# Weighted values of 64-wide heads with the probabilities stationary, the norm as a diagonal product, and reordered leading groups and gates

## The chip, the cores and the metric

The kernel runs on one core of one Trainium2 chip. The metric is the device time of one execution in microseconds (us), the median of three runs. The engines are TensorE (PE, with its weight loads as PEld), VectorE (DVE), ScalarE (ACT), GpSimd (POOL) and SyncE (SP), which here only issues DMAs.

## The reference

Two transformer blocks on 256 tokens of width 2048, all f32. The first block has two kinds of 64-wide attention heads side by side, sixteen each; each kind's 1024 outputs are normed together, and both go through one output matrix:

```python
h = rmsnorm(x, pre_mix_g[l]); proj = h @ w_in[l]
o_a = swa_sink_attention(q_a, k_a, v_a, sinks[l])         # 16 heads, 2 kv heads, window 128, sink in the sum
o_b = forgetting_attention(q_b, k_b, v_b, log_f)          # 16 heads, logit += c[t]-c[s], c = cumsum(log f)
o_a = rmsnorm(o_a.reshape(B, S, D_SWA), grp_swa_g[l])
o_b = rmsnorm(o_b.reshape(B, S, D_FOX), grp_fox_g[l])
mix = jnp.concatenate([o_a, o_b], axis=-1) @ w_out[l]
x = x + rmsnorm(mix, post_mix_g[l])                       # then a gated feed-forward with a short convolution
```

In both attentions a head's output is `p @ v` with `p = exp(s - m) / sum`. The second block mixes stick-breaking attention, a gated linear attention in chunks and a gated spatial unit, then attends to 256 memory rows, adds the residual and ends with a norm of x.

## The kernel before

**Layout.** Activations lie feature-major, as (128, k-tile, 256 tokens). A big product splits activations and weights into a high and a low f32r half and sums three of the four partial products: for one k-tile and one tile of 128 outputs, a product of 256 columns with the low weights (line 248) and one of 512 columns with the high weights (line 249). A group is two tiles over 16 k-tiles; one k-tile of a group is one step. `as_chunk` (lines 281 to 283) makes outputs by token instead, three products a k-tile and half.

**Weights.** `WeightStream` loads units of up to 128x1024 into four raw buffers, all DMAs on SP. ACT copies the high half (line 110), DVE subtracts for the low half (line 117), and PE uses the unit two units later. A unit is four k-tiles of a group. A raw buffer is loaded again when DVE is done with it.

**Order.** One program order per engine is written out by hand: side work runs as Python generators (`push`, `step`), each advanced once every so many steps; `yield n` means n steps later. `drain` advances them with no step of the stream between. PSUM has two-buffer tags P (groups) and S (scores) and single banks T and O.

**Attention.** `attn64` (line 402) takes heads in pairs. Scores go to S (line 475), DVE adds the bias and takes the maximum (483), ACT exponentiates with the sum accumulated (416), DVE takes the reciprocal and scales the probabilities, 128 and 256 columns per head (424 to 427), PE transposes three 128x128 blocks into T (434), ACT copies them out (437). `values` then makes the head's output feature-major in O, values stationary (64 columns) and transposed probabilities moved:

```python
o = self.p("O")
for h in (h0, h0 + 1):
    r, pt = (h % 2) * 64, weighted.pop(h)
    nc.tensor.matmul(o[r:r + 64, 0:S], vf(h, 0), pt[:, 0:S], start=True, stop=False)
    nc.tensor.matmul(o[r:r + 64, P:S], vf(h, 1), pt[:, S:S + P], start=False, stop=True)
```

ACT copies O out (455) and squares it (463); POOL sums the squares (465). For the forgetting heads ("fox") the pairs run while their keys arrive, but the values of the second values chunk (`v_chunk(2)`, flag `foxv`) come last, so their eight pairs are released together, one step apart, in `mix_tail`.

**Norm.** `group_norm_split` (line 499) sums over partitions with products by ones (`rms`, 328), takes the inverse root on ACT and DVE, multiplies the eight tiles on DVE and POOL in turn (508), and splits each into halves (217, 225) for the output matrix. `mix_tail` runs three output groups over the first eight k-tiles, drains the side work, and goes on with the other eight.

**Gates.** `fox_gates` (line 719) makes the cumulated log gates with products into T (734 to 736), copies them (738), transposes them into T (742), writes them to DRAM and reads them back broadcast over partitions with two 1 MB DMAs, all on POOL's queue (746, 750). POOL also scales the queries (317) and makes the biases (715).

**Other places.** The second block's first two groups (`w_gqk`) run one after the other, right after the residual and norm of the feed-forward (`residual_norm`, DVE lines 788, 789, 225). The gated linear attention masks 128x128 products into one array, per level first one diagonal block and then the other (1121 to 1133). At the start the norm gains come by a DMA on POOL (572) after 16 warm-up products (618). At the end POOL sums the last squares, the last norm is made by token (360, 368 to 378) and spread again by products (385), and line 1372 multiplies.

Of the kernel before, what the change touches and what calls it, by code (L numbers as in the profile page):

```python
# [16 lines left out]
P = 128  # L17
S = 256
# [130 lines left out]
class Kern:  # L149
# [151 lines left out]
    def join(self, ps, ntile=2):  # L301

        nc = self.nc
        e1 = self.t((P, 2, S), "e1")
        e2 = self.t((P, 2, S), "e2")
# [49 lines left out]
    def by_square(self, sqs):  # L355

        ps = self.p("T")
        for half in range(2):
            for i, sq in enumerate(sqs):
                self.nc.tensor.matmul(ps[:, half:half + 1], sq[:, half * P:(half + 1) * P], self.ones[:, 0:1],  # L360
                                      start=i == 0, stop=i == len(sqs) - 1)
        return ps[:, 0:2]

# [38 lines left out]
    def attn64(self, pairs, qf, kf, vf, bias, sink, oraw, acc, pts, n_pts, ready, vready=None):  # L402
# [6 lines left out]
        weighted = {}  # L409

        def pair(i, scs, sms):
# [29 lines left out]
        def values():  # L441

            n = len(pairs)
            order = [2 * (h // 2) for p in pairs for h in p]
            order = sorted(set(order), key=lambda h: max(i for i, p in enumerate(pairs) if h in p or h + 1 in p))
            for i, h0 in enumerate(order):
                while not (h0 in weighted and h0 + 1 in weighted and (vready is None or self.ready[vready])):
                    yield 1
                o = self.p("O")
                for h in (h0, h0 + 1):  # L450
                    r, pt = (h % 2) * 64, weighted.pop(h)
                    nc.tensor.matmul(o[r:r + 64, 0:S], vf(h, 0), pt[:, 0:S], start=True, stop=False)
                    nc.tensor.matmul(o[r:r + 64, P:S], vf(h, 1), pt[:, S:S + P], start=False, stop=True)
                n_done[0] += 2
                nc.scalar.activation(oraw()[:, h0 // 2, :], o[:, 0:S], AF.Copy)
                if i < 2:
                    sq = acc[i]
                elif i < n - 1:
                    sq = self.t((P, S), "tc")
                else:  # L460
                    nc.vector.tensor_tensor(out=acc[0], in0=acc[0], in1=acc[1], op=ALU.add)
                    sq = acc[1]
# [36 lines left out]
    def group_norm_split(self, oraw, acc, gi, dst):  # L499
# [24 lines left out]
    def setup(self):  # L524
# [37 lines left out]
        wide("w_gqk")  # L562
# [9 lines left out]
        nc.gpsimd.dma_start(self.gain0, a["gain0"])  # L572
        self.exp_tables()

    def block1_mix(self):
# [23 lines left out]
        acca = [V[0][:, o + i * S:o + (i + 1) * S] for i in (1, 2)]  # L599
        accb = [V[1][:, o + P + i * S:o + P + (i + 1) * S] for i in (0, 1)]  # L600
# [56 lines left out]
        oa = self.t((P, 8, S), "B5")  # L657
# [15 lines left out]
        def fox():  # L673
# [5 lines left out]
            def result():  # L679
                if not ob:  # L680
                    ob.append(self.t((P, 8, S), "X0"))
# [3 lines left out]
                                   accb, pts, 15, "fox", "foxv")  # L685
            yield from self.group_norm_split(ob[0], accb, 8, dst)

        for g in range(4):
            ps = self.ws_group(x) if g else psq
            self.push(self.scaled(ps, qa[:, 2 * g:2 * g + 2, :], rq, "swa", 4))  # L690
            if g == 0:
                fg = self.push(self.fox_gates(V), 2)
                side = self.push(chain(
                    self.attn64(order, qf, kf, va, self.alibi, sink, lambda: oa, acca, pts_a, 5, "swa"),
                    self.group_norm_split(oa, acca, 0, dst), fox()), 8)
# [23 lines left out]
    def fox_gates(self, V):  # L719
# [13 lines left out]
        ps = self.p("T")  # L733
# [5 lines left out]
        yield 4  # L739
        ps = self.p("T")  # L740
# [211 lines left out]
    def scaled_late(self, ps, dst, which):  # L952
        e = self.join(ps)
# [5 lines left out]
    def block2_mix(self):  # L959
# [101 lines left out]
    def gla(self, G0, G1, gr, V, tg):  # L1061
# [41 lines left out]
        def level(l):  # L1103
# [17 lines left out]
            for s_, t_, slot in ((0, 0, 0), (1, 1, 2)) if l < 8 else ((0, 1, 1),):  # L1121
                pss = [self.p("S", bufs=2) for r in range(2)]
                for h in range(4):
                    nc.tensor.matmul(pss[h % 2][:, h // 2 * P:(h // 2 + 1) * P], rows(k_, h)[:, s_ * P:(s_ + 1) * P],
                                     rows(q_, h)[:, t_ * P:(t_ + 1) * P], start=True, stop=True)
                for r in range(2):
                    ps3 = pss[r][:, 0:S].rearrange("p (h t) -> p h t", h=2)
                    a2 = at.rearrange("p (j r) c t -> p j r c t", r=2)[:, :, r, slot, :]
                    if l < 8:
                        nc.vector.copy_predicated(a2, gm[:, l, :].unsqueeze(1).broadcast_to([P, 2, P]), ps3)  # L1130
                    else:
                        nc.vector.tensor_copy(a2, ps3)
                yield 2
# [108 lines left out]
    def resid_evac(self, ps, g, acc, gname):  # L1242
# [5 lines left out]
        if gname == "final":  # L1248
            yield 2
            self.sq_acc(acc, Rg, g == 0)  # L1250
# [13 lines left out]
    def block2_cross(self):  # L1264
# [85 lines left out]
        for t in range(2):  # L1350
# [11 lines left out]
            if t == 0:  # L1362
                nc.scalar.activation(Rt, Rt, AF.Copy, scale=self.col("final", 14))
# [143 lines left out]
```

## Time and profile before

| | |
|---|---|
| Median of 3 runs | 1664.18 us (1663.37 to 1664.45) |
| The profiled execution's own time | 1668.66 us |
| Its span, first to last instruction | 1667.0 us |
| Mean granted TensorE clock | 0.993 |
| PE, PEld busy | 1638.9 us, 1434.2 us |
| DVE, ACT, POOL busy | 1084.0, 934.8, 329.5 us |
| DMA | 303.29 MB, mean 182 GB/s |

The profile is of one execution. A plain f32 product appears as two records, one of f32r as one, each with a weight load. Matmuls are pipelined, so a record's duration is longer than its spacing to the next: the cost on PE is read from the starts. A row gives start, duration, engine, line, operation, output and inputs, shape, count, and in brackets the engine's idle time ahead of it and what ended it. In this program bank T and bank O are single, so a product into one waits for the last reader of what was there.

### The profile page before, as it was taken

How to read it: one execution, taken by the hardware profiler on the slowest of the kernel's cores; microseconds unless marked ns; L12 is line 12 of the kernel's file. 1: busy time of each engine (PE TensorE's matmuls, PEld its weight loads, DVE VectorE, ACT ScalarE, POOL GpSimd, SP SyncE). 2: the span in 40 equal slices, each digit the busy share in tenths (PEclk: the TensorE clock that was granted, in tenths of full speed). 3: DMA queues.
4: the chain of work that ended last, by engine and by line, in shares of the span. 5: the costliest groups of instructions: out<-in, count | busy, mean ns of one | idle time of the engine just before them, and what ended most of it. 6: DMA issues, size and time to landing. Idle time of an engine off the chain costs nothing. (4 is left out here: it accounts for less than half of the span.)

```text
span 1667.0 us, 25018 instructions
## 1 busy us (share of the span) xinstructions
PE 1638.9 (98%) x9458; PEld 1434.2 (86%) x9458; DVE 1084.0 (65%) x1578; ACT 934.8 (56%) x1470; POOL 329.5 (20%) x270
## 2 busy tenths in 40 slices
PE   9899999999999999999999999998999999999997
PEld 8688887888888888888888888887989888888896
DVE  5677775568777777777774444448664655666766
ACT  6565565746555555555554444445545666655655
POOL 0344642211122212221220000001110322210112
PEclk9999999999999999999999999999999999999998
DMA  8545443746555555555555555654645544456652
GB/s 305 178 129 173 158 163 130 234 150 210 194 188 193 186 192 189 192 186 194 187 193 190 189 185 190 207 180 159 189 141 177 186 144 158 168 189 207 224 165 106
DMA packets 88393, 303.29 MB, mean 182 GB/s; under 512 B 9888, under 2 KB 10320, under 8 KB 87760
## 3 DMA queue, kind: packets, MB, share of 16 engines
q1 hardware_dynamic: 86976, 296.53, 52.2%
q0 software_dynamic: 1152, 4.76, 0.9%
q8 instruction: 74, 1.21, 0.3%
q14 instruction: 47, 0.39, 0.1%
q10 hardware_dynamic: 144, 0.40, 0.1%
HBM read 298.75 MB, written 2.90 MB: 181 GB/s over the span
## 5 line engine op out<-in xcount | busy, mean ns | idle before, releaser
L117 DVE TENSOR_TENSOR wl<-wr,wh 128x1024 fp32r<-128x1024 f32 (+4 forms) x546 | 687.9, 1262 | 337.3 <-ACT wh L110 336.5
L110 ACT ACTIVATE wh<-wr 128x1024 fp32r<-128x1024 f32 (+4 forms) x546 | 562.0, 1030 | 533.1 <-PE P L249 366.5
L249 PE MATMUL P<-X,wh 128*128 128x512 f32 x1852 | 649.3, 392 | 0.0
L249 PE MATMUL P<-B,wh 128*128 128x512 f32 x1668 | 590.2, 395 | 2.6 <-ACT B L217 1.4
L248 PE MATMUL P<-X,wl 128*128 128x256 f32 x1852 | 522.9, 282 | 1.4 <-ACT wh L110 1.3
L248 PE MATMUL P<-B,wl 128*128 128x256 f32 x1668 | 473.3, 284 | 1.9 <-DVE wl L117 1.9
L249 PEld LDWEIGHTS P<-X,wh 128*128 128x128 f32 x1852 | 348.5, 188 | 73.6
L249 PEld LDWEIGHTS P<-B,wh 128*128 128x128 f32 x1668 | 314.3, 188 | 74.3 <-DVE B L225 1.9
L248 PEld LDWEIGHTS P<-X,wl 128*128 128x128 f32 x1852 | 348.7, 188 | 7.0 <-issue 2.2
L248 PEld LDWEIGHTS P<-B,wl 128*128 128x128 f32 x1668 | 314.7, 189 | 5.8 <-DVE wl L117 1.7
L900 POOL TENSOR_TENSOR e<-e,rb 128x512 f32<-128x512 f32 x44 | 94.6, 2151 | 397.2 <-DVE e L309 382.3
L309 DVE TENSOR_TENSOR e<-P,e 128x512 f32<-128x512 f32 x93 | 64.2, 691 | 154.1 <-ACT e L308 150.0
L399 POOL TENSOR_TENSOR acc<-acc,tc 128x512 f32<-128x512 f32 x18 | 26.7, 1482 | 275.3 <-ACT tc L398 275.3
L281 PE MATMUL P<-wh,B 128*128 128x412 f32 (+2 forms) x192 | 68.7, 358 | 0.0
L905 ACT ACTIVATE tc<-e,cols 128x256 f32<-128x256 f32 x88 | 48.3, 597 | 34.1 <-POOL e L900 34.1
L282 PE MATMUL P<-wl,B 128*128 128x412 f32 (+2 forms) x192 | 65.0, 339 | 0.0
L283 PE MATMUL P<-wh,B 128*128 128x412 f32 (+2 forms) x192 | 65.0, 338 | 0.0
L308 ACT ACTIVATE e<-P 128x512 f32<-128x512 f32 x93 | 54.1, 582 | 9.0 <-PE P L249 6.9
L910 DVE SCALAR_TENSOR_TENSOR tc<-e,cols,tc 128x254 f32<-128x254 f32 x88 | 42.6, 484 | 3.1
L245 PE MATMUL P<-X,wh 128*128 128x512 f32 x116 | 43.5, 398 | 0.0
L908 DVE SCALAR_TENSOR_TENSOR tc<-e,cols,tc 128x255 f32<-128x255 f32 x88 | 41.8, 475 | 1.8 <-ACT tc L905 1.8
L281 PEld LDWEIGHTS P<-wh,B 128*128 128x128 f32 x192 | 36.1, 188 | 2.7 <-issue 0.3
(310 smaller groups left out, 1609.7 us busy)
## 6 DMA issues: line engine op xcount, KB each, us to landing
wr<-w_up SPq DMA_DIRECT2D x176, 512.0 KB, 4.4
wr<-w_down SPq DMA_DIRECT2D x88, 512.0 KB, 4.5
wr<-w_out SPq DMA_DIRECT2D x64, 512.0 KB, 4.5
wr<-w_qkb SPq DMA_DIRECT2D x32, 512.0 KB, 3.7
wr<-w_sb SPq DMA_DIRECT2D x32, 512.0 KB, 3.6
wr<-w_gate SPq DMA_DIRECT2D x32, 512.0 KB, 3.7
wr<-w_v SPq DMA_DIRECT2D x24, 412.0 KB, 3.2
wr<-w_v SPq DMA_DIRECT2D x16, 414.0 KB, 3.6
```

The source lines that it names most:

```text
L110: k.nc.scalar.activation(h[:, :n], src, AF.Copy)
L117: self.k.nc.vector.tensor_tensor(out=l[:, :n], in0=src, in1=h[:, :n].bitcast(F32), op=ALU.subtract)
L245: mm(o, wh, xf, start=True, stop=False)
L248: mm(o[:, 0:S], wl, xk[:, 0, :], start=False, stop=False)
L249: mm(o, wh, xf, start=False, stop=last)
L281: mm(o, xh, hh, start=kt == 0, stop=False)
L282: mm(o, xh, ll, start=False, stop=False)
L283: mm(o, xl, hh, start=False, stop=kt == KT - 1)
L308: nc.scalar.activation(e1[:, t0:t1, :], p[:, 0:t1 - t0, S:2 * S], AF.Copy)
L309: nc.vector.tensor_tensor(out=e2[:, t0:t1, :], in0=p[:, 0:t1 - t0, 0:S], in1=e1[:, t0:t1, :], op=ALU.add)
L900: nc.gpsimd.tensor_tensor(out=e, in0=e, in1=self.rb2(self.r2), op=ALU.mult)
L905: nc.scalar.activation(y[:, t, :], e[:, t, :], AF.Identity, scale=w(t, 2), bias=w(t, 3))
```

## The change

It has six parts. (1) `attn64` keeps the probabilities unscaled and stationary; a pair of heads makes six products of 64 columns, by token, into O; DVE scales by the reciprocals on the way out; one step later ACT squares each half with the sum accumulated, writing into the same bank. (2) `group_norm_split` makes the inverse root by token, puts it on a diagonal, and transposes and norms at once by 16 products with that diagonal, into T and O in turn. (3) `fox_gates` uses O, waits more steps, and issues its DMAs on SP. (4) The two leading groups of the second block take weight units alternately, their results joined straight into place. (5) The linear attention fills both diagonal blocks from one batch of products. (6) The gains come by SP; the last norm sums squares by `rms`, and the last tiles are scaled after it.

```diff
-            for sm, mx in sms:
+            for (sm, mx), h in zip(sms, heads):
                 if sink is not None:
                     nc.vector.tensor_tensor(out=mx[:, 4:6], in0=mx[:, 4:6], in1=mx[:, 6:8], op=ALU.add)
-                nc.vector.reciprocal(mx[:, 0:2], mx[:, 4:6])
-                for c, (x0, x1) in enumerate(blk):
-                    nc.vector.tensor_scalar(out=sm[:, x0:x1], in0=sm[:, x0:x1], scalar1=mx[:, c:c + 1], scalar2=None,
-                                            op0=ALU.mult)
+                nc.vector.reciprocal(rec[:, :, h], mx[:, 4:6])
...
                 o = self.p("O")
-                for h in (h0, h0 + 1):
-                    r, pt = (h % 2) * 64, weighted.pop(h)
-                    nc.tensor.matmul(o[r:r + 64, 0:S], vf(h, 0), pt[:, 0:S], start=True, stop=False)
-                    nc.tensor.matmul(o[r:r + 64, P:S], vf(h, 1), pt[:, S:S + P], start=False, stop=True)
+                oh = o[:, 0:S].rearrange("p (a h f) -> p a h f", a=2, h=2)
+                for j, h in enumerate((h0, h0 + 1)):
+                    pt = weighted.pop(h)
+                    nc.tensor.matmul(oh[:, 0, j, :], pt[:, 0:P], vf(h, 0), start=True, stop=True)
+                    nc.tensor.matmul(oh[:, 1, j, :], pt[:, P:2 * P], vf(h, 0), start=True, stop=False)
+                    nc.tensor.matmul(oh[:, 1, j, :], pt[:, 2 * P:3 * P], vf(h, 1), start=False, stop=True)
                 n_done[0] += 2
-                nc.scalar.activation(oraw()[:, h0 // 2, :], o[:, 0:S], AF.Copy)
...
-                nc.scalar.activation(sq, o[:, 0:S], AF.Square)
-                if 2 <= i < n - 1:
-                    nc.gpsimd.tensor_tensor(out=acc[i % 2], in0=acc[i % 2], in1=sq, op=ALU.add)
+                ot = oraw()[:, :, h0 * 64:h0 * 64 + P]
+                nc.vector.tensor_tensor(out=ot.rearrange("p a (h f) -> p a h f", h=2), in0=oh,
+                                        in1=rec[:, :, h0:h0 + 2].unsqueeze(3).broadcast_to([P, 2, 2, 64]),
+                                        op=ALU.mult)
                 yield 1
+                for half in range(2):
+                    nc.scalar.activation(o[:, S + half * P:S + (half + 1) * P], ot[:, half, :], AF.Square,
+                                         accum_out=ssq[:, half, i:i + 1])
...
-        yield 3
-        rb = self.rms(acc, 1024, "rb")
-        yield 1
-        for i in range(9):
-            if i < 8:
-                eng = nc.gpsimd if i % 2 else nc.vector
-                eng.tensor_tensor(out=oraw[:, i, :], in0=oraw[:, i, :], in1=rb, op=ALU.mult)
-            if i > 0:
-                self.split(dst(gi + i - 1), oraw[:, i - 1, :], self.col("grp", gi + i - 1))
-            yield 1 if gi else 4
+        yield 2
+        r = self.t((P, 2), "grs")
+        nc.vector.tensor_reduce(out=r, in_=ssq, axis=AX.X, op=ALU.add)
+        _, dg = self.rms_tok(r, 1024, "grc")
+        yield 4
+        for i in range(0, 8, 2):
+            ps = self.p("TO"[i // 2 % 2])
+            for j in range(2):
+                for half in range(2):
+                    c = (2 * j + half) * P
+                    nc.tensor.matmul(ps[:, c:c + P], oraw[:, half, (i + j) * P:(i + j + 1) * P], dg[:, half, :],
+                                     start=True, stop=True)
+            for j in range(2):
+                self.split(dst(gi + i + j), ps[:, j * S:(j + 1) * S], self.col("grp", gi + i + j))
+            yield 3 if gi else 8
...
-        nc.gpsimd.dma_start(self.gain0, a["gain0"])
...
             nc.sync.dma_start(R[:, kt, :], a["xT"][:, kt, :])
+            if kt == 0:
+                nc.sync.dma_start(self.gain0, a["gain0"])
...
-        ps = self.p("T")
+        ps = self.p("O")
...
-        yield 4
-        ps = self.p("T")
+        yield 8
+        ps = self.p("O")
...
-        nc.gpsimd.dma_start(dr, ct)
+        yield 4
+        nc.sync.dma_start(dr, ct)
+        yield 6
...
-            nc.gpsimd.dma_start(self.N[i].rearrange("p a b -> p (a b)"), src)
+            nc.sync.dma_start(self.N[i].rearrange("p a b -> p (a b)"), src)
...
-        for dst, w in ((gq, "rq"), (gk, "rb")):
-            ps = self.ws_group(x)
-            self.push(self.scaled_late(ps, dst, w))
+        pss = [self.big(), self.big()]
+        for i in range(0, KT, 4):
+            for ps, dst, w in ((pss[0], gq, "rq"), (pss[1], gk, "rb")):
+                self.ws_sub(ps, x, list(range(i, i + 4)), (0, KT - 1))
+                if i == KT - 4:
+                    self.push(self.scaled_late(ps, dst, w, dst))
...
-            for s_, t_, slot in ((0, 0, 0), (1, 1, 2)) if l < 8 else ((0, 1, 1),):
-                pss = [self.p("S", bufs=2) for r in range(2)]
+            blocks = ((0, 0), (1, 1)) if l < 8 else ((0, 1),)
+            n = len(blocks)
+            pss = [self.p("S", bufs=2) for r in range(2)]
+            for i, (s_, t_) in enumerate(blocks):
                 for h in range(4):
...
-                yield 2
+            yield 2
...
-        rc, dg = self.rms_tok(self.by_square(sqs), D, "rb1c")
-        nc.scalar.activation(Rt, Rt, AF.Copy, scale=self.col("final", 15))
-        rb = self.t((P, S), "rb")
-        nc.vector.tensor_copy(rb, self.by_row(dg))
+        sqs[2:2] = [self.sq_last[:, 0, :], self.sq_last[:, 1, :]]
+        rb = self.rms(sqs, D, "rb")
+        for t in range(12, KT):
+            nc.scalar.activation(self.R[:, t, :], self.R[:, t, :], AF.Copy, scale=self.col("final", t))
```

## Rows read from the trace of the kernel before

**Rows 1.** The page, part 1: busy time, share of the span, instructions.

```profile
PE 1638.9 (98%) x9458; PEld 1434.2 (86%) x9458; DVE 1084.0 (65%) x1578; ACT 934.8 (56%) x1470; POOL 329.5 (20%) x270
```

**Rows 2.** The waits of PE: line, what it waited for; total us, times, longest.

```profile
PE S L475 <- POOL B L317: 3.2, 1, 3.2
...
PE T L434 <- DVE acc L744: 1.7, 1, 1.7
...
PE T L434 <- DVE fc L738: 1.4, 1, 1.4
...
PE O L452 <- ACT B L463: 0.8, 1, 0.8
```

**Rows 3.** Busy time in one stretch; after POOL the granted clock, DMA share, GB/s.

```profile
71.20:77.40 6.20, 6.19 (x25) 4.97 (x26) 2.77 (x11) 0.96 (x2) 2.98 (x2) 0.50 0.81 316
```

**Rows 4.** PE in order of time, 264 to 266.3 us (start, us, engine, line).

```profile
264.46 0.40 PE L249 MATMUL P<-B,wh 128*128 128x512 f32 x1
...
264.81 0.40 PE L249 MATMUL P<-B,wh 128*128 128x512 f32 x1
265.05 1.02 PE L328 MATMUL O<-B,ones 128*128 128x256 f32 x4
...
266.02 0.39 PE L249 MATMUL P<-B,wh 128*128 128x512 f32 x1
```

**Rows 5.** PE in order of time, one pair of weighted values, 255 to 257 us.

```profile
255.19 0.39 PE L249 MATMUL P<-B,wh 128*128 128x512 f32 x1
255.52 0.66 PE L452 MATMUL O<-B,B 128*64 128x256 f32 x4
...
256.32 0.39 PE L248 MATMUL P<-B,wl 128*128 128x256 f32 x1
256.55 0.39 PE L249 MATMUL P<-B,wh 128*128 128x512 f32 x1
```

**Rows 6.** PE in order of time, the gates' narrow products, 55 us.

```profile
55.12 0.37 PE L735 MATMUL T<-fz,ones 128*128 128x16 f32 x2
55.34 0.38 PE L736 MATMUL T<-fz,cp 128*128 128x16 f32 x2
```

**Rows 7.** PE in order of time, the first norm's products, 43 us.

```profile
43.28 0.61 PE L385 MATMUL O<-td,ones 128*128 128x128 f32 x4
43.70 0.50 PE L245 MATMUL P<-X,wh 128*128 128x512 f32 x1
```

**Rows 8.** ACT in order of time, the square of the pair in rows 5.

```profile
256.73 0.38 ACT L463 ACTIVATE tc<-O 128x256 f32<-128x256 f32 x1
```

**Rows 9.** Groups by line, shapes apart, 45 to 280 us: busy us, mean ns of one.

```profile
L416 ACT ACTIVATE sm<-sm,mx 128x128 f32<-128x128 f32 x32 | 12.4, 389 | 0.0
...
L309 DVE TENSOR_TENSOR e<-S,e 128x256 f32<-128x256 f32 x1 | 0.4, 411 | 0.0
```

**Rows 10.** PE in order of time, 278 us, after the drain of `mix_tail`.

```profile
278.00 0.36 PE L248 MATMUL P<-X,wl 128*128 128x256 f32 x1 [1.26 <-ACT wh L110]
```

**Rows 11.** PE in order of time: first leading product, and the one 31 steps later.

```profile
1127.87 0.58 PE L245 MATMUL P<-B,wh 128*128 128x512 f32 x1
...
1157.86 0.59 PE L328 MATMUL O<-acc,ones 128*128 128x256 f32 x2
```

**Rows 12.** DVE in order of time, leading groups: two of its weight splits.

```profile
1131.14 1.22 DVE L117 TENSOR_TENSOR wl<-wr,wh 128x1024 fp32r<-128x1024 f32 x1
...
1142.09 1.21 DVE L117 TENSOR_TENSOR wl<-wr,wh 128x1024 fp32r<-128x1024 f32 x1
```

**Rows 13.** PE in order of time, one batch of the masked products, 1198 us.

```profile
1197.99 0.35 PE L283 MATMUL P<-wh,B 128*128 128x414 f32 x1
1198.27 0.72 PE L1124 MATMUL S<-B 64*128 64x128 f32 x8
...
1199.21 0.35 PE L282 MATMUL P<-wl,B 128*128 128x414 f32 x1
```

**Rows 14.** ACT in order of time, the first split of x.

```profile
6.04 0.51 ACT L217 ACTIVATE X<-R,gain 128x256 fp32r<-128x256 f32 x1 [3.53 <-DMA gain<-gain]
```

More of the change, by code (lines that the diff above doesn't have):

```diff
@@ L299, in as_chunk, with join @@
         return ps
-    def join(self, ps, ntile=2):
+    def join(self, ps, ntile=2, e2=None):
         nc = self.nc
         e1 = self.t((P, 2, S), "e1")
-        e2 = self.t((P, 2, S), "e2")
+        e2 = self.t((P, 2, S), "e2") if e2 is None else e2
         parts = [(t, t + 1, ps[t].unsqueeze(1)) for t in range(ntile)] if isinstance(ps, list) else [(0, ntile, ps)]
@@ L353, in by_token @@
         return rc
-    def by_square(self, sqs):
-        ps = self.p("T")
[L358 to L362, printed above, removed]
     def rms_tok(self, ssq, n, tag):
@@ L399, in sq_acc, with attn64 @@
             nc.gpsimd.tensor_tensor(out=acc, in0=acc, in1=sq, op=ALU.add)
-    def attn64(self, pairs, qf, kf, vf, bias, sink, oraw, acc, pts, n_pts, ready, vready=None):
+    def attn64(self, pairs, qf, kf, vf, bias, sink, oraw, ssq, pts, n_pts, ready, vready=None):
         nc = self.nc
@@ L409, in attn64 @@
         weighted = {}
+        rec = self.t((P, 2, 16), "rec")
         def pair(i, scs, sms):
@@ L441, in values @@
         def values():
-            n = len(pairs)
             order = [2 * (h // 2) for p in pairs for h in p]
@@ L561, in setup @@
         units += xv[0:2]
-        wide("w_gqk")
+        for i in range(2):
+            for half in range(2):
+                for g in range(2):
+                    units.append((a["w_gqk"][2 * g + i][:, 1024 * half:1024 * half + 1024], [1024], False))
         for c in range(5):
@@ L598, in block1_mix @@
         ka = V[0][:, o:o + S]
-        acca = [V[0][:, o + i * S:o + (i + 1) * S] for i in (1, 2)]
-        accb = [V[1][:, o + P + i * S:o + P + (i + 1) * S] for i in (0, 1)]
+        ssqa, ssqb = [V[1][:, o + 16 * i:o + 16 * i + 16].rearrange("p (a b) -> p a b", a=2) for i in range(2)]
         def v_evac(ps, ci):
@@ L656, in block1_mix @@
         qa = self.t((P, 8, S), "B0")
-        oa = self.t((P, 8, S), "B5")
+        oa = self.t((P, 2, 8 * P), "B5")
         order = []
@@ L680, in result @@
                 if not ob:
-                    ob.append(self.t((P, 8, S), "X0"))
+                    ob.append(self.t((P, 2, 8 * P), "X0"))
                 return ob[0]
             yield from self.attn64([(h, h + 1) for h in range(0, 16, 2)], qfb, kfb, vb, self.fox_bias, None, result,
-                                   accb, pts, 15, "fox", "foxv")
-            yield from self.group_norm_split(ob[0], accb, 8, dst)
+                                   ssqb, pts, 15, "fox", "foxv")
+            yield from self.group_norm_split(ob[0], ssqb, 8, dst)
         for g in range(4):
@@ L693, in block1_mix @@
                 side = self.push(chain(
-                    self.attn64(order, qf, kf, va, self.alibi, sink, lambda: oa, acca, pts_a, 5, "swa"),
-                    self.group_norm_split(oa, acca, 0, dst), fox()), 8)
+                    self.attn64(order, qf, kf, va, self.alibi, sink, lambda: oa, ssqa, pts_a, 5, "swa"),
+                    self.group_norm_split(oa, ssqa, 0, dst), fox()), 8)
         v_chunk(1)
@@ L949, in block1_ffn, with scaled_late @@
         self.nc.gpsimd.dma_start(self.vxd, vx)
-    def scaled_late(self, ps, dst, which):
-        e = self.join(ps)
+    def scaled_late(self, ps, dst, which, e2=None):
+        e = self.join(ps, e2=e2)
         yield 6
@@ L1120, in level @@
                 yield 2
-            for s_, t_, slot in ((0, 0, 0), (1, 1, 2)) if l < 8 else ((0, 1, 1),):
-                pss = [self.p("S", bufs=2) for r in range(2)]
+            blocks = ((0, 0), (1, 1)) if l < 8 else ((0, 1),)
+            n = len(blocks)
+            pss = [self.p("S", bufs=2) for r in range(2)]
+            for i, (s_, t_) in enumerate(blocks):
                 for h in range(4):
-                    nc.tensor.matmul(pss[h % 2][:, h // 2 * P:(h // 2 + 1) * P], rows(k_, h)[:, s_ * P:(s_ + 1) * P],
+                    c = (h // 2 * n + i) * P
+                    nc.tensor.matmul(pss[h % 2][:, c:c + P], rows(k_, h)[:, s_ * P:(s_ + 1) * P],
                                      rows(q_, h)[:, t_ * P:(t_ + 1) * P], start=True, stop=True)
[L1126 to L1132, printed above, removed]
-                yield 2
+            for r in range(2):
+                ps4 = pss[r][:, 0:2 * n * P].rearrange("p (h c t) -> p h c t", h=2, c=n)
+                a2 = at.rearrange("p (j r) c t -> p j r c t", r=2)[:, :, r]
+                if l < 8:
+                    nc.vector.copy_predicated(a2[:, :, 0:3:2, :],
+                                              gm[:, l, :].unsqueeze(1).unsqueeze(1).broadcast_to([P, 2, 2, P]), ps4)
+                else:
+                    nc.vector.tensor_copy(a2[:, :, 1:2, :], ps4)
+            yield 2
             left[0] -= 1
@@ L1249, in resid_evac @@
             yield 2
-            self.sq_acc(acc, Rg, g == 0)
+            if g < 6:
+                self.sq_acc(acc, Rg, g == 0)
+            else:
+                self.sq_last = self.t((P, 2, S), "tc")
+                nc.scalar.activation(self.sq_last, Rg, AF.Square)
+                return
             yield 1
```

12 lines of the change are left out of this document (1 added, 11 removed).

## The prediction

> **What bounds the kernel now.** I read the busy shares first, then who TensorE (PE) waited for, then the order of its instructions around each edit, then the engines that feed it there. PE is busy 98% of the span [rows 1], so its own work sets the time: a product added anywhere lengthens the kernel by its spacing, work taken off VectorE (DVE), ScalarE (ACT) or GpSimd (POOL) is worth nothing unless PE waits for it, and gains can only be in the few waits. The largest ones with a name are the first three lines of [rows 2], all at the start of the attention: 3.2 + 1.7 + 1.4 = 6.3 us. After the last of them PE ran 6.2 us at a granted clock of 0.50, the 1.2 GHz level [rows 3]. The sum is made against the profiled execution's own 1668.66 us; the median of the three runs is 1664.18, and I carry the difference over to it. About 0.2% (3.3 us) is what a measurement of this kernel can tell from no change.
>
> A step below is one k-tile of a two-tile group: two pairs of products, 0.35 us a pair (264.81 - 264.46) [rows 4], so 0.70 us.
>
> **Weighted values, PE.** Now a pair of heads costs 256.55 - 255.19 = 1.36 us between two products of the stream, 0.35 of which is the stream's own: 1.01 us [rows 5]. After the change a pair is 6 products of 64 moved columns, each two records like every plain f32 product here: 12 records, each with a 128x128 stationary operand of its own. No row shows 64 columns. Records that move 16 columns are 0.11 us apart (two in 55.34 - 55.12) [rows 6], those that move 128 are (43.70 - 43.28)/4 = 0.105 apart [rows 7]. Both sides agree, so 12 x 0.11 = 1.33 us: +0.32 a pair, 16 pairs, +5.1 us. The moved columns fall by four, but the loads of the stationary operand set the pace.
>
> The Trainium skill, TensorE: Matmul & The Clock Gate, section Back-to-back issue gap, gives about 81 ns for a sustained load-and-product pair at 128 columns; by that a pair would cost 0.97 us and the 16 pairs some 5.7 us less than I sum. The trace measures 0.105 to 0.11 [rows 6, 7], so I keep that.
>
> **Weighted values, the bank.** All pairs use the single bank O. Now ACT copies and squares, and the bank is free at 256.73 + 0.38 = 257.11 [rows 8], 0.79 us after PE went on to the next step at 256.32 [rows 5]; one step nearly covers that. After, the chain that frees the bank is longer: product to DVE 0.15 (an estimate, like the other handovers); the scaled copy of 128x256 out of PSUM 0.41, the join of that size; handover 0.05; two ACT squares of 128 columns with accumulation, 0.39 each, the size of the exponentials [rows 9], with 0.1 for the second's accumulator read; 0.1 back to PE: 1.6 us. The squares are issued only just ahead of the next pair's products, which write the same bank. In the forgetting heads all eight pairs come one step apart, since their values chunk is last; 1.6 against 0.70 makes PE wait 0.9 us seven times. Now that stretch is 8 x 1.01 + 7 x 0.70 + 0.8 for one wait on ACT's square [rows 2] = 13.8 us; after, 8 x 1.33 + 7 x 1.6 = 21.8: **+8.0 us**, 2.6 of it counted above. Bounds: +2.6 if the chain is hidden, +11 if half the gaps also meet a weight split on DVE. The sliding-window pairs come in four twos with two steps between: 8 x 0.32 + 4 x 0.2 = **+3.4** (2.6 to 6). What goes (64 + 64 DVE scalings, POOL's sums of squares) is off PE's path and worth nothing by itself.
>
> **Norm and transpose by a diagonal product.** Each group: 16 f32 products of 128 columns, 32 records x 0.11 = 3.55 us on PE. They replace two products with ones, (266.02 - 264.81) - 0.35 = 0.86 us [rows 4]. Twice +2.7, and PE now stands in line for the diagonal (a sum, logarithm, exponent, seven short DVE instructions, with four steps or 2.8 us as cover): 0.5 for both, 0 to 2.6. **+5.9** (5.4 to 8). The 1.26 us wait for a weight copy [rows 10] goes, as ACT no longer queues eight splits behind POOL's multiplies: **-1.3** (0 to -1.6).
>
> **Gates in another bank, their DMAs on SP.** The second and third wait of [rows 2] are for bank T, held by the gates until DVE reaches their copies; the first is for POOL's scaling of the queries, queued behind POOL's DMA that waits for its own write to DRAM. With bank O, idle there until the first weighted values, and with SP's queue, all three go, and so does the slow stretch: 6.3 + half of 6.2 = **-9.4** (-5 to -9.6). Late next would be the scores' queries, which by the order of the program are scaled just before use. On SP one write and two 1 MB broadcasts now stand ahead of weight loads; the four raw weight buffers cover that, and what it costs without them is rival 5.
>
> **Leading groups side by side.** PE takes 1157.86 - 1127.87 = 29.99 us for 31 steps [rows 11] that need 21.7: 8.3 lost. DVE is what is late: it makes the normed x and the low halves of the weights in one queue. The new order asks for x half as fast, but step for step DVE's queue stays as it is: the low half that the second unit needs ends at 1131.14 + 1.22, the one that the fifth needs at 1142.09 + 1.21 = 1143.30 [rows 12] (the second and the fifth split of that stretch). Four units of four steps follow: 1143.3 + 11.2 = 1154.5, against 1157.86 + 0.70 = 1158.6 now: **-4.1** (-1 to -8.3).
>
> **Masked products two blocks at once.** One batch of eight records costs 1199.21 - 1197.99 = 1.22 us less 0.38 for two products of 414 columns (0.35 for 768 [rows 4]): 0.84 [rows 13], of which four concurrent pairs x 0.105 = 0.42 is work. Eight batches merge into others: 8 x 0.42 = **-3.4** (-1 to -4).
>
> **Ends.** The first split waits 3.53 us for the gains, which come by POOL's queue [rows 14]; by SP's, just behind the first x tile, I let them land 0.7 sooner: **-0.7** (0 to -1.5; each later load starts a little later). At the end two scalings and a chain of small instructions leave the path, but 12 records of 0.22 us come in (0.86 for four [rows 4]): **-0.6** (+0.5 to -1.2).
>
> **Sum.** +8.0 + 3.4 + 5.9 = +17.3; -9.4 - 4.1 - 3.4 - 1.3 - 0.7 - 0.6 = -19.5. Net -2.2: 1666.5 for such a profiled execution, **1662.0 for the median**. Large terms nearly cancel, so the forecast is no change to slightly faster, 1657 to 1667.
>
> **Rivals.**
> 1. *The bank's chain hides* (15%). For: today's chain on the same bank all but fits one step. Against: two more handovers. Then 5.4 us less: 1656.6.
> 2. *Spacing is not set by the load* (3%). If records took 0.055 us, a quarter of a 256-column record's 0.22, each pair would cost 0.66 less, in the burst too: 16 x 0.66 = 10.6 less, 1651.4. [rows 6] speak against it: 16 columns cost as much as 128.
> 3. *The clock falls in the burst* (10%), slower. Place: the eight pairs of the forgetting heads, where PE would be idle 0.9 us in every 2.9. Price: at the 0.50 of [rows 3] the 1.33 us of a pair doubles; seven pairs take 9 us more, 1671; slower from about four such pairs on. For: PE fell to 0.50 after the idle time of [rows 2]. Against: these idle times are shorter, with products between.
> 4. *Loads and products don't overlap* (2%). In this kernel a record would cost its load, 0.11, plus its columns, 0.05 for 64 and 0.11 for 128: 192 x 0.05 + 64 x 0.11 = +17 us, 1679. The Trainium skill, TensorE: Matmul & The Clock Gate, section Measured speedup vs the span model, says that a load overlaps a running product only in another row group. By that rule the records of [rows 7] would be 0.22 apart; they are 0.105.
> 5. *The gates' waits come back* (10%): SP holds the weights back, or the first scores still wait for their queries. With a third of the 9.4 left as gain: 1668.3.
>
> **Chances.** The forecast has the remaining 60%; its spread of some 3 us around 1662.0 lies across the line of 1660.85. Faster: 0.6 x 0.4 + 0.18 = 0.42; slower: 0.6 x 0.05 and most of rivals 3 to 5, 0.18; the same 0.40. The range takes in rivals 1 and 5 and leaves out 2, 4 and most of 3: 1655 to 1669.
>
> **What would show it.** Right: no PE wait in the attention's first 40 us, clock 1.00 there; 12 records 0.11 us apart for each pair; in the burst a wait of 0.9 us for ACT's square ahead of each pair, periods of 2.9; 16 products in four groups for each norm; a few waits of 0.4 to 1.7 us for DVE's low halves in the leading groups, which end 4 us sooner. Wrong: burst periods near 2.0 (rival 1) or a clock below 1.00 in it (rival 3), records closer than 0.1 (rival 2) or 0.16 apart (rival 4), waits for POOL, SP or bank O before the first weighted values (rival 5).

## The result and the profile after

The changed kernel takes 1683.1 us (median of 5 runs, 1674.26 to 1684.56) against 1664.18 (median of 5, 1663.37 to 1666.77): ratio 1.0102 (the quotient of the two medians is 1.0114), 95% interval 1.0075 to 1.013. It is slower by 1%, outside the range that I gave. The five runs differ by the mean clock that they were granted: the one of 1674.26 had 0.996, the others 0.987 to 0.989. The profiled execution took 1684.56 us, its span is 1682.9: 15.9 more than before.

Part 1 of the page, to be read beside [rows 1], and the first waits of PE, beside [rows 2] (line, what it waited for: total us, times, longest):

```profile
PE 1654.9 (98%) x9570; PEld 1460.6 (87%) x9570; DVE 1068.7 (64%) x1507; ACT 939.1 (56%) x1502; POOL 309.6 (18%) x247
```

```profile
PE O L442 <- ACT O L452: 9.5, 8, 1.9
PE P L245 <- DVE e L887: 3.9, 1, 3.9
PE P L282 <- DVE wl L117: 1.1, 3, 0.5
```

DVE is busy 15 us less, POOL 20 us less, and nothing came of it; PE is busy 16 us more. The three waits of [rows 2] at the start of the attention are gone. In their place stand waits of the value products (L442) for ACT's squares into bank O (L452), and one of 3.9 us for DVE's copy of the memory values (L887). The busy time by stretch from 236 us on, with the granted clock:

```profile
core 0: us, PE busy (x) PEld busy (x) DVE busy (x) ACT busy (x) POOL busy (x), PEclk, DMA share, GB/s
236.00:248.00 12.00, 12.00 (x74) 11.37 (x73) 8.39 (x26) 7.33 (x19) 4.83 (x8) 1.00 0.59 197
248.00:254.40 6.40, 4.88 (x36) 4.21 (x35) 2.25 (x5) 3.52 (x12) 0.00 (x0) 1.00 0.59 203
254.40:271.50 17.10, 14.44 (x58) 12.48 (x58) 2.41 (x4) 5.00 (x19) 0.00 (x0) 0.50 0.09 33
271.50:278.30 6.80, 4.30 (x31) 3.57 (x30) 0.85 (x2) 2.55 (x9) 0.00 (x0) 1.00 0.00 0
278.30:285.20 6.90, 6.84 (x26) 6.26 (x27) 1.81 (x4) 0.82 (x5) 0.00 (x0) 0.51 0.16 51
```

The burst, the eight pairs of the forgetting heads' values, begins at 248. PE idles for 1.52 us of the first 6.4, all of it in one wait ahead of the second pair, then its clock is at 0.50 (1.2 GHz) for 17.1 us, and once more for 6.9. The stretch in order of time shows what each wait is:

```profile
250.33 0.40 PE L249 MATMUL P<-B,wh 128*128 128x512 f32 x1
252.24 0.43 PE L442 MATMUL O<-B,B 128*128 128x64 f32 x2 [1.51 <-ACT O L452]
...
253.83 0.43 DVE L447 TENSOR_TENSOR X<-O,rec 128x256 f32<-128x256 f32 x1 [2.51 <-PE O L444]
254.15 0.40 PE L249 MATMUL P<-B,wh 128*128 128x512 f32 x1
254.35 0.28 ACT L452 ACTIVATE O<-X 128x128 f32<-128x128 f32 x1 [2.16 <-DVE X L447]
254.56 0.19 ACT L452 ACTIVATION_READ_ACCUMULATOR O<-X 128x1 f32 x1
254.78 0.28 ACT L452 ACTIVATE O<-X 128x128 f32<-128x128 f32 x1
255.00 0.19 ACT L452 ACTIVATION_READ_ACCUMULATOR O<-X 128x1 f32 x1
255.24 0.50 PEld L442 LDWEIGHTS O<-B,B 128*128 128x128 f32 x2 [1.02 <-ACT O L452]
...
260.02 1.06 ACT L110 ACTIVATE wh<-wr 128x1024 fp32r<-128x1024 f32 x1 [0.79 <-PE P L249]
260.98 0.26 ACT L452 ACTIVATE O<-X 128x128 f32<-128x128 f32 x1
...
261.86 0.48 PE L442 MATMUL O<-B,B 128*128 128x64 f32 x1 [1.88 <-ACT O L452]
```

At 255.24 the products start when ACT's second square is done, 0.87 us after the stream's last product had ended its share of PE (254.15 + 0.22). At 261.86 the squares stood behind a weight split of ACT (260.02), and PE waited 2.1 us by the same count; the 1.88 in brackets counts from the end of a record, which lasts longer than its share.

A product of the weight stream can be found in both traces by its number in the stream (8640 in each), so its delay against before can be followed. The table gives what each stage added (us, profiled executions), beside the forecast's terms; the columns after "changed" are experiments of the next section.

| stage, up to (us of before) | forecast | changed | e1 | e2 | e3 | e14 |
|---|---|---|---|---|---|---|
| start, 45 | -0.7 | -0.28 | -0.58 | -1.17 | +0.02 | -0.65 |
| gates, 79 | -9.4 | -9.07 | -9.07 | -9.07 | -8.92 | -9.05 |
| first attention, 148 | +3.4 | +8.79 | +3.30 | +8.71 | 0.00 | +3.28 |
| its norm, 228 | +2.95 | +1.96 | +1.93 | +1.93 | 0.00 | +1.97 |
| burst, its norm, the copy wait, 292 | +9.65 | +21.03 | +3.82 | +12.65 | -0.02 | +3.81 |
| leading groups, 1172 | -4.1 | -1.94 | -2.65 | -2.58 | -1.91 | -4.10 |
| masked products, 1293 | -3.4 | -3.23 | -3.22 | -3.22 | -3.23 | -3.22 |
| behind them, 1640 | 0 | -0.92 | 0.00 | -1.02 | -0.98 | -0.01 |
| end | -0.6 | -0.41 | -0.43 | -0.42 | -0.38 | -0.42 |
| span | -2.2 | +15.9 | -6.9 | +5.8 | -15.4 | -8.4 |

The 0.9 to 1.0 us "behind them" is one wait that the profile of before has and some others haven't; e5 below, with the code of before there, lost it too, so it isn't the change.

### The profile page after: what moved, and what is told of

It is laid out like the page before. It is cut to its first block, busy times and chain, and to the rows that moved or that the text cites. A ratio compares the mean times of both kernels' runs of the same rounds, so it can differ in the third digit from the quotient of the medians.

```text
span 1682.9 us, 25168 instructions
## 1 busy us (share of the span) xinstructions
PE 1654.9 (98%) x9570; PEld 1460.6 (87%) x9570; DVE 1068.7 (64%) x1507; ACT 939.1 (56%) x1502; POOL 309.6 (18%) x247
## 5 line engine op out<-in xcount | busy, mean ns | idle before, releaser
L249 PE MATMUL P<-B,wh 128*128 128x512 f32 x1668 | 591.5, 396 | 0.1
L245 PE MATMUL P<-B,wh 128*128 128x512 f32 x100 | 39.3, 415 | 4.2 <-DVE e L887 3.9
```

What stands on the lines that cost most here:

```text
L245: mm(o, wh, xf, start=True, stop=False)
L249: mm(o, wh, xf, start=False, stop=last)
```

## The experiments

Theory: the chain on the single bank O (products, DVE's copy, two squares written into the same bank) makes PE idle about once per pair, and this idle time lets the clock fall. Rival: the 64-column products, limited by their weight loads, let it fall by themselves. The times of e10 and e11 are medians of two runs, all others of at least four; the kernel before took 1665.5 to 1666.8 beside them.

**e1, the squares written elsewhere.**

```diff
-nc.scalar.activation(o[:, S + half * P:S + (half + 1) * P], ot[:, half, :], AF.Square,
+sq = self.t((P, S), "tc")      # ahead of the loop over the halves
+nc.scalar.activation(sq[:, half * P:(half + 1) * P], ot[:, half, :], AF.Square,
```

> The changed kernel with one thing altered: ScalarE writes the squares of the weighted values to a tile in SBUF and no longer into the second half of bank O, so that the bank is free again when VectorE has made its scaled copy. Theory A (the bank's chain makes TensorE idle in the burst, and that idle time lets the granted clock fall): from the last product to the free bank it is then about 0.2 + 0.42 + 0.05 = 0.67 us beside a step of 0.70, so the waits on ScalarE's squares (9.5 us in the profile) go, the clock stays at 1.00 from 245 to 290 us, and the loss between 246 us and the end of the norm falls from 21.0 to about 7 us: the time 1683 - 14 = 1669 us (1663 to 1673). Rival B (the narrow 64-column products, which are limited by their loads, let the clock fall by themselves): the waits go, but the clock falls all the same, and the time stays at 1676 or above.

Measured 1662.27 us, ratio to before 0.9969 (0.9959 to 0.998): 21 us less than the changed kernel, more than theory A asked: its 14 us counted the burst alone, and 5.5 more came back in the first attention (table). What is left of bank O among the waits of PE, and the burst:

```profile
PE O L442 <- DVE X L447: 0.6, 1, 0.6
```

```profile
244.00:260.10 16.10, 15.46 (x121) 14.43 (x121) 5.22 (x10) 8.18 (x33) 0.00 (x0) 1.00 0.29 93
```

The clock stays at 1.00 with the same narrow products, and the stage costs 3.82 in place of 21.03. So these products by themselves don't bring it down.

**e2, the waits filled with work.** The bank's chain stays; ahead of each pair but the first of the burst:

```diff
+for _ in range(4):
+    nc.tensor.matmul(f, d[:, 0, 0:P], d.rearrange("p a b -> p (a b)"), start=True, stop=True)
```

> The changed kernel with four more 512-column products (0.88 us, their result is not used) ahead of the value products of each pair but the first of the second attention; bank O and its chain stay as they are. They stand where TensorE waits now. Theory A (idle time lets the clock fall): most of each wait is filled with work, the clock stays at 1.00 through the burst or falls later, and the time comes down although TensorE does 6.2 us more: about 1683 - 10 = 1673 us (1668 to 1677). Rival B (the narrow products let the clock fall): the clock falls as before and the filling costs up to 6 us on top: 1683 to 1689 us. Rival C (the waits alone are the loss and the clock does not matter): no change, 1683.

Measured 1675.28, ratio 1.0051 (1.0036 to 1.0066): 8 us faster than the changed kernel with 6 us more work on PE, so rivals B and C both fail. The clock stood at 1.00 from 236 to 285 us (one stretch of it below); of the waits on the squares six were left, three in the first attention, as in the changed kernel, and three in the burst, none over 1.2 us:

```profile
PE O L446 <- ACT O L456: 5.4, 6, 1.2
```

```profile
248.00:264.00 16.00, 14.46 (x99) 12.47 (x99) 4.39 (x7) 6.71 (x22) 0.00 (x0) 1.00 0.25 84
```

Of this stage's 12.65 us 3.82 are what e1 has too and 6.2 the added products; the 2.6 that remain are about the three waits in the burst (2.5), with nothing for the clock.

**e5 and e9, idle time in the kernel before.** Its wide value products stay; ACT holds bank O longer, with two added squares per pair of the burst (e5) or six (e9), which nothing reads:

```diff
 nc.scalar.activation(sq, o[:, 0:S], AF.Square)
+if vready is not None:
+    for _ in range(2):
+        nc.scalar.activation(o[:, S:2 * S], o[:, 0:S], AF.Square)
```

> The kernel before, unchanged but for two more ScalarE squares of bank O per pair of the second attention, written into the bank's other half (0.39 us each, not used): the bank is held as long as in the changed kernel, about 0.2 + 4 x 0.39 + 0.1 = 1.9 us beside a step of 0.70, and no product is added or made narrower. Theory A (idle time of about 1 us per pair lets the granted clock fall, whatever the products are): seven waits of about 1.1 us, 8 us in all, less the 2 us that the burst waits already, and the clock at 0.50 over a part of the 15 us from 250 us: 13 to 20 us slower than the kernel before. Rival B (it needs the 64-column products as well): the clock stays at 1.00 and the loss is the waits alone, 5 to 8 us.

Measured 1669.7, ratio 1.002 (1.001 to 1.0029). The chain came out shorter than I had reckoned: 0.4 to 0.7 us of idle time for six of the seven pairs and 1.6 for one, the stage 3.79 slower, the clock at 1.00:

```profile
248.00:264.00 16.00, 12.07 (x87) 7.78 (x87) 1.90 (x3) 11.61 (x32) 3.97 (x5) 1.00 0.25 80
```

That misses both numbers and doesn't test theory A, so e9 went further.

> e5_before_bank_held with six added squares of bank O per pair instead of two: there the chain came to 1.5 us and TensorE waited only 0.5 to 0.8 us a pair. Four more squares add about 1.1 us, so seven waits of about 1.7 us, 12 us in all, with the wide products of the kernel before. Theory A (idle time lets the clock fall, whatever the products are): the clock stands at 0.50 over a good part of the burst, and the stretch costs 16 to 25 us against the kernel before. Rival B (it needs the 64-column products as well): the clock stays at 1.00 and the stretch costs the waits alone, 9 to 13 us.

Measured 1686.89, ratio 1.0122 (1.0107 to 1.0137); the stage costs 17.2 us.

```profile
PE O L452 <- ACT O L466: 14.1, 7, 3.1
```

```profile
248.00:256.70 8.70, 3.77 (x29) 2.44 (x28) 0.94 (x1) 6.80 (x21) 0.00 (x0) 1.00 0.31 101
256.70:263.50 6.80, 4.43 (x18) 2.62 (x16) 1.23 (x1) 5.78 (x17) 1.45 (x2) 0.50 0.15 45
263.50:277.20 13.70, 6.85 (x48) 4.46 (x49) 1.00 (x2) 10.60 (x30) 2.17 (x3) 1.00 0.05 18
277.20:280.60 3.40, 3.40 (x13) 2.93 (x11) 0.65 (x1) 2.23 (x7) 0.00 (x0) 0.50 0.41 133
```

With the old products and idle time alone the clock falls to 0.50, twice. Narrow products aren't needed for it. But these waits, 0.9 to 3.1 us by the profile's count, are longer than the changed kernel's five (0.7 to 1.9), and they are most of the 17.2 us; the clock took about 3.9, half of the 4.43 + 3.40 us that PE was busy at 0.50.

**e13, half of the chain.** Of each pair's two squares only the first is written to bank O.

> The changed kernel with only the second of a pair's two squares moved to SBUF; the first is still written into bank O. The chain is then about 0.2 + 0.42 + 0.1 + 0.45 = 1.2 us, so TensorE waits about 0.5 us per pair in the burst (4 us in all, with one or two longer where ScalarE is at a weight split), as in e5_before_bank_held, but here between 64-column products. Theory A (what counts is the length of the waits): the clock stays at 1.00 as in e5, and the time is 1662 + 4 = 1666 us (1665 to 1669). Theory B (the narrow products bring the point nearer at which the clock falls): it falls in the burst although the waits are no longer than in e5, 1671 to 1680 us.

Measured 1671.29, ratio 1.0033 (1.0023 to 1.0044), the stage 11.1 slower, by theory B's number but not by its mechanism. Two of the seven waits met a weight split of ACT and were 1.6 us long, the others 0.4 and one 1.25, and the clock fell only behind the last:

```profile
246.70:268.40 21.70, 16.82 (x120) 14.24 (x119) 5.10 (x11) 7.95 (x33) 0.00 (x0) 1.00 0.18 64
268.40:271.80 3.40, 3.40 (x13) 2.91 (x12) 1.37 (x3) 0.70 (x4) 0.00 (x0) 0.50 0.30 76
```

PE idles for 4.9 of the 21.7 us, and the clock takes half of 3.4: 1.7. Those two are most of the 7.3 us that the stage loses against e1, and 2.3 more are lost in the first attention, where no clock falls. Whether narrow products bring the fall nearer stays open.

**e10 and e11, the price of a value product.** From e1: e10 leaves the third product of each head out (the second then closes the sum), e11 makes each as two of 32 columns.

```diff
-nc.tensor.matmul(oh[:, 1, j, :], pt[:, 2 * P:3 * P], vf(h, 1), start=False, stop=True)      # e10
```
```diff
+for f in (slice(0, 32), slice(32, 64)):                                                      # e11
+    nc.tensor.matmul(oh[:, 0, j, f], pt[:, 0:P], vf(h, 0)[:, f], start=True, stop=True)
...
```

> e1_squares_elsewhere with the third of each head's value products left out (the weights of the second half of the keys are not used): 8 records a pair in place of 12. Theory (each record costs 0.11 us on TensorE's path, since nothing else binds once the bank is free early): 16 pairs x 4 x 0.11 = 7.0 us less, about 1655 us. Rival (VectorE's and ScalarE's work of a pair sets the pace, not the products): less than 3 us.

> e1_squares_elsewhere with each 64-column value product made as two of 32 columns: the same columns in all, twice the records and weight loads. Theory (the price of a record is that of its weight load, whatever its columns): 24 records a pair, 12 x 0.11 = 1.3 us more, 16 pairs: 21 us more, about 1683 us. Rival (the columns set the price): within 3 us of e1_squares_elsewhere, 1662 us.

Measured 1655.69 (6.6 less than e1) and 1681.87 (19.6 more). Records of 32 columns in e11:

```profile
254.53 0.39 PE L445 MATMUL O<-B,B 128*128 128x32 f32 x2
254.76 0.39 PE L443 MATMUL O<-B,B 128*128 128x32 f32 x2
254.98 0.39 PE L444 MATMUL O<-B,B 128*128 128x32 f32 x2
```

Two records every 0.22 us: 0.11 each, half the columns and the same price.

**e3, the attention and norm of before; e12, e6, e7, the gates.** e3 is the changed kernel with `attn64`, `group_norm_split` and their layouts taken back. e12 takes back `fox_gates` as well; e6 puts back its bank alone, e7 its queue alone:

```diff
-ps = self.p("O")                       # e6, twice
+ps = self.p("T")
-nc.sync.dma_start(dr, ct)              # e7, all three transfers
+nc.gpsimd.dma_start(dr, ct)
```

> The changed kernel with the attention and the group norm of the kernel before (scaled probabilities, values by column, the norm on VectorE and GpSimd); gates, leading groups, masked products, start and end stay as changed. Theory A: the whole loss lies in the new attention (6.4 us with the first attention, about 2.9 with its norm, 21.0 in the burst), and the rest gains 7.9 up to the end of the gates, 1.8 in the leading groups, 3.2 in the masked products, 1.3 at the end: 1664.2 - 14 = 1650 us (1648 to 1654). Rival (the gates gain only because the new attention loads VectorE less, so part of the 7.6 us comes back): 1655 to 1660 us.

> e3_old_attention with the products of the gates again in bank T, that the transposes of the first attention want; the gates' transfers stay on SyncE's queue. Theory (both parts of the gates' change matter: the bank frees the transposes, the queue frees GpSimd's alibi and so the scores): about half of the 9 us of this stretch comes back, 4 to 5 us slower than e3_old_attention. Rival (all of it is GpSimd's queue): no change from e3_old_attention, within 1 us.

> e3_old_attention with the gates' three transfers again on GpSimd's queue; their products stay in bank O. Theory (both parts matter): the wait of the scores on GpSimd comes back, 3 to 5 us with the time at half the clock behind it, so 3 to 5 us slower than e3_old_attention. Rival (it is the bank alone): no change from e3_old_attention, within 1 us.

> e3_old_attention with the gates wholly as in the kernel before: products in bank T, transfers on GpSimd's queue, the old places in the order. e6 and e7 put back one of the two each and gave back 1 us and nothing. Theory (either part alone avoids the waits that come in a row and let the clock fall there): with both back the 8 to 9 us of this stretch come back whole, about 1661 to 1662 us, and the clock is at 0.50 near 71 us as in the kernel before. Rival (the gain of that stretch comes from the earlier start, the gain0 transfer on SyncE, and not from the gates): it stays at 1653 us.

e3: 1653.17, ratio 0.9916 (0.9899 to 0.9932). Without the new attention the rest gains 13.6 us (15.4 in the span), as the table adds it up. e6: 1654.57, e7: 1653.14: 1.4 and nothing given back, where I expected 3 to 5 from each. e12: 1660.43, ratio 0.9964 (0.995 to 0.9978): 7.3 us come back, and with them the first three waits of [rows 2] and the slow clock:

```profile
PE S L466 <- POOL B L317: 3.1, 1, 3.1
PE T L425 <- DVE acc L739: 1.7, 1, 1.7
PE T L425 <- DVE fc L733: 1.4, 1, 1.4
```

```profile
66.00:71.60 5.60, 2.53 (x19) 1.83 (x17) 2.89 (x9) 3.18 (x12) 2.37 (x3) 1.00 0.52 166
71.60:75.00 3.40, 3.40 (x13) 2.79 (x12) 2.77 (x11) 0.49 (x1) 2.12 (x2) 0.50 0.98 381
```

So the parts don't add. With bank T back alone, the waits for T return in part (1.4 and 0.7) but neither the one for POOL nor the slow clock; with POOL's queue back alone, none does. Both keep the new places in the order (the longer delays ahead of the transposes and the transfers), which e12 takes back as well; what these places bring alone wasn't tried.

**e4, e8, e14, the second leading group in the S banks.** In the changed kernel both groups ask for a P bank at once, and the memory values still hold one. PE, DVE and ACT there:

```profile
1153.04 0.40 PE L249 MATMUL P<-B,wh 128*128 128x512 f32 x1
1153.57 1.22 DVE L117 TENSOR_TENSOR wl<-wr,wh 128x1024 fp32r<-128x1024 f32 x1
1154.71 0.68 DVE L785 TENSOR_TENSOR X<-X,rb 128x512 f32<-128x512 f32 x1
1155.43 0.69 DVE L786 TENSOR_TENSOR R<-R,X 128x512 f32<-128x512 f32 x1
1156.03 0.88 DVE L225 SCALAR_TENSOR_TENSOR B<-R,cols,B 128x256 fp32r<-128x256 f32 x2
1156.83 0.48 DVE L887 TENSOR_SCALAR e<-P,rmc 128x256 f32<-128x256 f32 x1
1157.36 0.79 PE L245 MATMUL P<-B,wh 128*128 128x512 f32 x1 [3.92 <-DVE e L887]
```

The copy that frees the bank (L887) is the last of five things in DVE's queue.

```diff
-pss = [self.big(), self.big()]
+pss = [self.big(), self.spare()]
```

> The changed kernel with the second leading group summed in the two S banks and not in the second P bank, which VectorE still has to empty of the memory values when the group wants it. Theory A (the P bank costs the leading groups their gain): the wait of 3.9 us on VectorE goes, the clock does not fall at 1155.6 us, and the leading groups gain about 4 us more than now: 1683.1 - 4 = 1679 us. Rival (the waits for the normed tiles are only moved: TensorE then waits at the next k-tiles for VectorE and ScalarE, whose queues are full there): 1682 to 1684 us.

> e3_old_attention with the second leading group in the two S banks, as in e4_lead_spare_banks. The leading groups gain about 2 us more than in e3_old_attention, as e4 showed against the changed kernel (3.9 in place of 1.7 by the trace): about 1651 us where e3_old_attention is 1653, the fastest of all. Rival: the shift is given back behind (the graph's normalisation waits for other banks and VectorE), within 0.5 us of e3_old_attention.

> The changed kernel with both repairs, the squares in SBUF (e1) and the second leading group in the S banks (e4): the new attention at its best. The two stages lie 850 us apart, so the gains should add: 1662.3 - 1.3 = 1661 us, still 9 us above e8_old_attention_spare_banks (1651.7), the price of the narrow products themselves. Rival (a stage behind gives one of them back): 1662 us or above.

e4 (on the changed kernel): 1681.93, ratio 1.0094 (1.0077 to 1.011). The wait is gone and the stage gains 4.1 by the trace in place of 1.9, but the times overlap those of the changed kernel, so the run alone doesn't show it. e8 (on e3): 1651.74, ratio 0.991 (0.9892 to 0.9929), 1.4 under e3: the fastest of all, 14 us under the kernel before. Its runs and e3's just touch (1651.35 to 1652.2, 1652.02 to 1653.27); by the trace the stage gains 2.1 more than in e3. e14 (on e1): 1660.06, ratio 0.9956 (0.9939 to 0.9972), 2.2 under e1, as expected, and 8.3 over e8: what the new attention costs with both repairs.

## Why the prediction was wrong

**The step that failed is the price of the bank's chain**, "makes PE wait 0.9 us seven times", taken at a clock of 1.00. The chain itself was right where nothing stood in its way: from the end of one pair's products (253.60, where the stream's next one starts) to the next pair (255.24) 1.64 us, forecast 1.6, made of 0.23 to DVE, 0.43 for its copy, 0.09 to ACT, 0.84 for the two squares and 0.05 back. Ahead of three of the seven pairs it took longer, 2.5 to 4.0 us, as the copy met a weight split of DVE once and the squares one of ACT twice (my upper bound had such splits, on DVE alone; the 4.0 has three transposes in it too). Even so PE's idle time in the burst is 6.7 us where 7 x 0.9 makes 6.3. But the idle time let the clock fall, as e1, e2 and e9 show from three sides. The stage lost 21.03 against 9.65. Of that 3.82 stays without the waits (e1; my terms without them, 2.6 + 2.95 - 1.3, give 4.25). The other 17.2 splits by the table of stretches into about these two: PE was busy 14.44 + 6.84 us at half clock, 10.6 lost; idle 1.52 + 2.66 + 2.50 = 6.7.

**Rival 3 was what happened**, and I gave it 10%. Its place was right. Its price of 9 us was near the 10.6 by luck: it counted seven pairs of value products at half clock, where four and part of a fifth ran so (5.4 us), and left out the transposes, the stream's steps between them and the steps behind the burst, which ran at half clock too. The reason given against it, "these idle times are shorter, with products between", doesn't hold: the fall at 254.4 us stands 2.2 us behind the end of a single wait of 1.7 us (250.55 to 252.24), the one in the first attention 1.4 us behind a single wait of 1.4. Yet a wait of 1.6 us in e5, and the first of the two in e13, had no fall behind them, so these runs don't tell which wait brings one. The Trainium skill, TensorE: Matmul & The Clock Gate, section A second HAM failure mode: psum-queue depth-cycling, tells of a like case, short idle times between groups of products that cycle through PSUM banks, with the clock swinging between its levels. The trace agrees (five waits of 0.7 to 1.9 us on one bank, the clock at 0.50 twice between 248 and 285 us), and it belonged beside rival 3.

**First attention**, +3.4 forecast, +8.79. The products were right: e1 has +3.30. The 0.2 for each of four waits was not: three were 1.4, 1.2 and 0.8 (by PE's share, as above), 3.4 together. In the first ACT was at a weight split when the squares came; I had looked for such splits on DVE. And 3.4 us at half clock behind it cost 1.7.

```profile
70.30 1.06 ACT L110 ACTIVATE wh<-wr 128x1024 fp32r<-128x1024 f32 x1 [2.31 <-PE P L249]
72.14 0.43 PE L442 MATMUL O<-B,B 128*128 128x64 f32 x2 [1.23 <-ACT O L452]
73.50:76.90 3.40, 3.40 (x13) 2.92 (x13) 0.88 (x5) 1.52 (x8) 0.00 (x0) 0.51 0.92 245
```

**Products.** 12 records a pair at 0.11: e10 takes four away and gains 6.6 where 16 x 4 x 0.11 is 7.0; e11 adds twelve and loses 19.6 of 21. Rivals 2 and 4 fall. The Trainium skill's 81 ns (TensorE: Matmul & The Clock Gate, section Back-to-back issue gap) are not seen in this kernel: 0.105 us at 128 columns [rows 7], 0.11 at 32 in e11's rows. What rival 4 takes from the Trainium skill stands in TensorE: Matmul & The Clock Gate, section The mechanism; the 0.105 us of [rows 7] speaks against it here.

**Norm.** +2.95 forecast, +1.96 for the first. The four groups cost 0.8 each (below), so 3.2 for 3.55, and PE didn't stand in line for the one below (288.32 + 0.22 = 288.54). With the 0.86 that goes this makes 2.3; the remaining 0.4 of the first norm isn't explained.

```profile
288.32 0.40 PE L249 MATMUL P<-B,wh 128*128 128x512 f32 x1
288.56 1.05 PE L499 MATMUL T<-td,X 128*128 128x128 f32 x8
289.37 0.48 PE L245 MATMUL S<-B,wh 128*128 128x512 f32 x1
```

**Gates.** -9.4 forecast, -9.07 measured, but the reason was only half right: I had given a wait to the bank and another to the queue, but with the new places either of the two brings nearly all (e6, e7). Some 1.5 of it is the profiled execution of before, whose slow stretch there was 6.8 us long; e12 and e5, with its gates, had 3.4.

**Leading groups.** -4.1 forecast, -1.94. The step "DVE's queue stays as it is" left out who holds the bank that the second group wants. With that repaired the number came out (-4.1), yet for a second reason as well: the profile of before had its clock at 0.50 from 1138.9 to 1145.8 us, which I had not looked for, and e5 and e9, with the same code there and no fall, are 2.1 faster than it.

```profile
1138.90:1145.80 6.90, 5.76 (x19) 4.58 (x18) 6.03 (x11) 3.19 (x6) 0.00 (x0) 0.51 0.43 155
```

So against a kernel before without this fall the reordering as changed is worth nothing (-1.94 + 2.1, with a fall of its own at 1155.6; e1 with its fall at 1135.1 has -0.5), and with the S banks about 2.

**Masked products, ends.** -3.4 and -0.6 forecast, -3.23 and -0.41. The start, -0.7 forecast, came to -0.28 and scatters by as much as its size (-1.17 to +0.02 in the table).

**The carried difference.** The median missed by 21.1 (1683.1 for 1662.0), the profiled execution by 18.1 (+15.9 for -2.2). The other 3.0 is a step of its own: the gains were read from an execution of 1668.66 us and carried over whole to a median of 1664.18, though part of them was that execution's own slow clock, in the gates and in the leading groups.

## What to carry to other kernels

On an engine that is busy 98% of the time a short repeated wait is priced twice, once as idle time and once as the clock that it may cost: price such a stretch at both clock levels and give the slower one a real chance. Free a PSUM bank at its first reader: scratch output that is written back into it ties it to a second engine's queue, here for 21 us. Work moved from idle engines to the full one, such as a norm made by products, costs its products and brings nothing (8 us here, the narrower value products included).

## What had not been expected of the hardware

The falls of the clock differ from execution to execution of one program. The leading groups of before ran at 0.50 for 6.9 us in its profile and at 1.00 in the profiles of e5 and e9, the same instructions; the runs of before beside e13 reach from 1662.77 (mean clock 0.996) to 1669.8 (0.992), those of the changed kernel from 1674.26 (0.996) to 1684.56 (0.987). A single profile of a kernel with idle places therefore carries several us of chance. And PE's records with a load of their own cost nearly the same, 0.10 to 0.11 us, with 16 and 128 [rows 6, 7], 32 (e11) and 64 moved columns.
